# Where the last loads of a one-core transformer layer land, and how its token tiles are finished

## The chip, the core and the metric

The kernel runs on one core of one Trainium2 chip. The time is the device time of one execution in microseconds (us), the median of three runs. The core has five engines that run their own instruction streams and wait for each other through semaphores: TensorE (PE, with its weight loads shown as PEld), VectorE (DVE), ScalarE (ACT), GpSimd (POOL) and SyncE (SP). SP and POOL issue nearly all transfers here, ACT a few. SBUF is the on-chip memory, PSUM the banks that TensorE writes to.

## The reference

One layer of a decoder: RMSNorm, one wide input projection, sparse attention and a gated MLP side by side, two projections up, an output projection, and at the end a gate with a per-layer embedding and a final RMSNorm. S is 512 tokens, D is 2048. What matters here is the end:

```python
x = x + merged @ w_out[l]
x = x + jax.nn.sigmoid(x @ w_ple_gate[l]) * (p[l] @ w_ple[l])
return rms_norm(x, final_g)          # x * rsqrt(mean(x*x)) * final_g
```

The matrix `w_ple_gate` is 2048 x 2048. Call x after the output projection x2, and p[l] @ w_ple the embedding term. The final norm needs the sum of squares of a whole row of 2048, so no part of a row can be written out before all four column groups of that row are there.

## The kernel before, in words

**Numbers as sums.** Matmuls run on pairs: every fp32 operand is split into a high part, rounded for TensorE, and a low part, the rest (`high` at L141 on ACT, `low` at L147 on DVE). One product of two tiles is three matmuls: high x high, high x low, low x high.

**Jobs.** All weight matmuls are a list of jobs that one generator, `gemm`, yields through matmul by matmul. The weights stream from HBM through a ring of three buffers named `raw` (512 KB each, two row blocks of 128); SP issues a load when the buffer's last reader, a `low` on DVE, is done. Before each step of a job `gemm` calls `flush` (work put off by one step), `split_to` (the splits of weights of coming steps) and `pop`. `pop` takes items from a queue `background`; how many per step is `state["pops"]`. So the order of DVE, ACT and POOL instructions among the splits is fixed by these queues when the program is built.

**The last three jobs** multiply x2 by `w_ple_gate`: `pg0` gives column group 0 of the gate (512 columns), `pg1` groups 1 and 2, `pg3`, the last job, group 3. `pg3` has 16 row blocks. Its first eight go step by step over all four token tiles (128 tokens each; lines L349 to L351). Its last eight, the *tail*, are kept whole in SBUF in tiles named `th` and `tl`, and the tail's matmuls (L366 to L368) run token tile by token tile: tile t=0 takes its 24 matmuls, then t=1, and so on. So the four token tiles finish one after the other, and `evac_last(ps, t)` is called when tile t is there.

**The gate and the final norm.** For a column group cg and token tile t, `ple_add` (L701 and L704) makes x2 + 0.5 (1 + tanh) embedding with two DVE instructions; a Square on ACT (L724, or L743 for group 3) adds up the squares. For groups 0, 1 and 2 this is `final_add(cg, t)`, an item of `background`. Group 3 is done in `evac_last`: tanh out of PSUM (L736), sums of the squares of the other groups (L739, L740), `ple_add`, Square, a Sqrt on ACT (L749), a reciprocal on DVE (L751), and then the four column groups are multiplied by that factor and by `final_g` and stored. Tanh and Sqrt need different function tables on ACT; a one-element activation on `warm` (L738, L765) loads the table ahead of use.

In the kernel before, t=0 and t=1 are finished together, after t=1 has come; they multiply by the factor and `final_g` in one DVE instruction per piece (L756). For t=2 and t=3 the multiplication by `final_g` (the tile `fg`) is done ahead of time: groups 0, 1 and 2 by POOL (`final_weigh`, L728, six calls), group 3 by DVE (L745); what is left is the factor alone (L762 on DVE, L759 on ACT).

**Late loads.** While `pg3` runs, five tiles of 1 MB each are loaded by POOL's queue: the x2 of groups 1 and 3, the embedding terms of groups 1 and 3, and `final_g`, one row of 8 KB repeated over the 128 partitions. Places: `fq` is a pool that is opened when the pool of job `pg1` closes. It holds `fg`, the x2 of groups 1 and 3 and the tail; the embedding of group 1 goes to the tile `x`, that of group 3 to a tile `s4` that group 0 has used. One item, `load_last`, issues three of the loads; it stands behind the four `final_add(2, t)`.

With one pop per step, the items are taken in this order: `final_add(2, 0..3)`, `load_last`, `final_add(1, 0..3)`, six `final_weigh`.

Of the kernel before, what the change touches and what calls it, by code (L numbers as in the profile page):

```python
# [13 lines left out]
F32 = mybir.dt.float32  # L14
F32R = mybir.dt.float32r
BF16 = mybir.dt.bfloat16
AF = mybir.ActivationFunctionType
ALU = mybir.AluOpType
# [3 lines left out]
P = 128  # L22
S = 512
D = 2048
TT = S // P
# [38 lines left out]
def kernel(ctx: ExitStack, tc: tile.TileContext, x, p, norm_g, w_in,  # L64
                      pe_k, w1_k, w2_k, pe_v, w1_v, w2_v, ln_g, ln_b, sgu_w, sgu_b,
                      w_up_a, w_up_b, w_out, w_ple, w_ple_gate, final_g, out):
    nc = tc.nc
    x, out = x[0], out[0]
    p = p[0, 0]
# [15 lines left out]
    eps_t = const.tile([P, 1], F32, name="eps_t")  # L85
    nc.gpsimd.memset(eps_t, EPS)
    warm = const.tile([P, 1], F32, name="warm")
# [74 lines left out]
    background = deque()  # L162
# [43 lines left out]
    state = {"loads": 0, "sum": 0, "high": 0, "low": 0, "ahead": 0, "more": 1, "pops": 2, "due": 0}  # L206
# [178 lines left out]
    def finish(name):  # L385
        while name not in done:
            next(run)
        flush()
# [95 lines left out]
    pl_in, ple_t = {}, {}  # L484
# [17 lines left out]
    def spilled(cg):  # L502
        return spill[:, 512 * cg:512 * cg + 512].rearrange("(t p) c -> p t c", p=P)
# [190 lines left out]
    f_tiles, x2_tiles, sg_tiles = {}, {}, {}  # L694
    ss = small[:, 48:64].rearrange("p (t c) -> p t c", t=TT)

    def place(tag, dtype):
        return actp.tile([P, 4, S], dtype, tag=tag, name="p_" + tag)

    def ple_add(cg, t, sg):  # L700
        nc.vector.scalar_tensor_tensor(out=sg, in0=sg, scalar=1.0, in1=ple_t[cg][:, t],  # L701
                                       op0=ALU.add, op1=ALU.mult)
        sl = x2_tiles[cg][:, t]
        nc.vector.scalar_tensor_tensor(out=sl, in0=sg, scalar=0.5, in1=sl, op0=ALU.mult, op1=ALU.add)  # L704
        return sl
# [15 lines left out]
    def final_add(cg, t):  # L721

        sl = ple_add(cg, t, sg_tiles[cg][:, t])
        deferred.append(lambda: nc.scalar.activation(sg_tiles[cg][:, t], sl, AF.Square, accum_out=ss[:, t, cg:cg + 1]))  # L724

    def final_weigh(cg, t):
        sl = x2_tiles[cg][:, t]
        nc.gpsimd.tensor_tensor(out=sl, in0=sl, in1=f_tiles["fg"][:, 512 * cg:512 * cg + 512], op=ALU.mult)  # L728

    def evac_last(ps, t):  # L730
        fg = f_tiles["fg"]
        if t == 0:
            f_tiles["rs"] = f_tiles["pool"].tile([P, TT, 2], F32, name="rs")
        r = f_tiles["rs"]
        sg = stream.tile([P, 512], F32, tag="hi", name="sg", bufs=4)
        nc.scalar.activation(sg, ps[t], AF.Tanh, scale=0.5)  # L736
        if t:
            nc.scalar.activation(warm, eps_t, AF.Sqrt)  # L738
        nc.vector.tensor_reduce(out=r[:, t, 0:1], in_=ss[:, t, 0:3], axis=AX.X, op=ALU.add)  # L739
        nc.vector.tensor_scalar(out=r[:, t, 0:1], in0=r[:, t, 0:1], scalar1=1.0 / D, scalar2=EPS,  # L740
                                op0=ALU.mult, op1=ALU.add)
        sl = ple_add(3, t, sg)
        nc.scalar.activation(sg, sl, AF.Square, accum_out=ss[:, t, 3:4])  # L743
        if t > 1:
            nc.vector.tensor_tensor(out=sl, in0=sl, in1=fg[:, 1536:], op=ALU.mult)  # L745
        if t == 0:
            return
        for i in range(0 if t == 1 else t, t + 1):
            nc.scalar.activation(r[:, i, 1:2], ss[:, i, 3:4], AF.Sqrt, bias=r[:, i, 0:1], scale=1.0 / D)  # L749
            rs = r[:, i, 0:1]  # L750
            nc.vector.reciprocal(rs, r[:, i, 1:2])  # L751
            for cg in (0, 2, 1, 3):
                c = slice(512 * cg, 512 * cg + 512)
                rows, o = out[i * P:i * P + P, c], x2_tiles[cg][:, i]
                if i < 2:
                    nc.vector.scalar_tensor_tensor(out=o, in0=o, scalar=rs, in1=fg[:, c], op0=ALU.mult, op1=ALU.mult)  # L756
                    nc.sync.dma_start(rows, o)
                elif t == TT - 1 and cg < 2:
                    nc.scalar.mul(o, o, rs)  # L759
                    nc.scalar.dma_start(rows, o)  # L760
                else:
                    nc.vector.tensor_scalar(out=o, in0=o, scalar1=rs, scalar2=None, op0=ALU.mult)  # L762
                    nc.sync.dma_start(rows, o)
        if t < TT - 1:
            nc.scalar.activation(warm, eps_t, AF.Tanh)  # L765

    def gate_act(p, k, t):
# [6 lines left out]
    add_job(Job("pg0", "N", w_ple_gate, 0, 512, KT, h_act, evac_first, zs))  # L774
    add_job(Job("pg1", "S", w_ple_gate, 512, 512, KT, gate_act, evac_quad(final_sg, place_sg), ("o", "s", "t")))
    add_job(Job("pg3", "N", w_ple_gate, 1536, 512, KT, h_act, evac_last, ("s", "s", "g", "g"), tail=8))

    run = gemm()
# [115 lines left out]
    with tc.tile_pool(name="cmp", bufs=1) as cmp:  # L894
# [32 lines left out]
        for m in range(16):  # L927
            o, st, sp = hid[m // 8], m % 8 == 0, m % 8 == 7
# [10 lines left out]
        t = o32[:, 4, 128:256].rearrange("p (g n) -> p g n", g=GROUPS)  # L939
        h = o32[:, 5].rearrange("p (g r n) -> p g r n", g=GROUPS, r=4)  # L940
        c = cmp.tile([P, 1], F32, name="hid_c")
        lo_r, up_r = slice(0, 64), slice(64, 128)
        for n, rows in enumerate((lo_r, up_r)):
            o, q = (t[rows].rearrange("p (s g n) -> p s g n", s=2, g=GROUPS)[:, n]
                    for t in (o32[:, 6, :8 * (NCMP + 2)], hid[1]))
            nc.vector.tensor_tensor(out=c[rows], in0=o[:, 0, NCMP:NCMP + 1], in1=q[:, 0, NCMP + 1:], op=ALU.add)
            nc.vector.scalar_tensor_tensor(out=y[rows], in0=o[:, :, :NCMP], scalar=c[rows], in1=q[:, :, 1:NCMP + 1],
                                           op0=ALU.add, op1=ALU.add)
# [374 lines left out]
    for hf in range(2):  # L1323
        b = bank("s", "ps_w")
        for j in range(4):
            nc.tensor.transpose(b[:, j * P:j * P + P], wn[hf][:, j], ident)
        nc.vector.tensor_tensor(out=ws[hf], in0=b.rearrange("p (g t) -> p g t", g=4),
                                in1=tri.unsqueeze(1).to_broadcast([P, 4, P]), op=ALU.mult)
# [9 lines left out]
    def new_s4(q, dtype=F32R):  # L1338
        t = s4p.tile([P, 4, S], dtype, tag=f"s4{q}", name=f"s4{q}")
        return t  # L1340
# [116 lines left out]
    def new_x(dtype=F32):  # L1457
        t = xp.tile([P, 4, S], dtype, tag="x", name="x")
        return t
# [55 lines left out]
    def columns(src, cg):  # L1515
        return src[:, 512 * cg:512 * cg + 512].rearrange("(t p) c -> p t c", p=P)
# [124 lines left out]
    def load_x2(cg, t):  # L1641
        x2_tiles[cg] = t
        nc.gpsimd.dma_start(t, columns(x2_dram, cg))

    def load_ple(cg, t):
        ple_t[cg] = t
        nc.gpsimd.dma_start(t, spilled(cg))
# [16 lines left out]
        flush()  # L1664
    ph_q.close()
    fq = f_tiles["pool"] = ctx.enter_context(tc.tile_pool(name="fq", bufs=1))
    fg = f_tiles["fg"] = fq.tile([P, D], F32, name="fg")
    tails = {i: fq.tile([P, 8, 512], F32R, name="t" + i) for i in "hl"}
    f_tiles["tail"] = lambda i, k: tails[i][:, k:k + 1]
    assert not background  # L1670
    for cg, t in ((1, new_x()), (3, new_s4(0, F32))):
        ple_t[cg] = t
    late = {cg: fq.tile([P, TT, 512], F32, name=f"x2_{cg}") for cg in (1, 3)}
    load_x2(1, late[1])
    load_ple(1, ple_t[1])
    state["pops"] = 1

    def load_last():
        nc.gpsimd.dma_start(fg, bass.AP(tensor=final_g.tensor, offset=final_g.offset, ap=[[0, P], [1, D]]))
        load_ple(3, ple_t[3])  # L1680
        load_x2(3, late[3])

    background.extend(lambda t=t: final_add(2, t) for t in range(TT))
    background.append(load_last)
    background.extend(lambda t=t: final_add(1, t) for t in range(TT))
    background.extend(lambda t=t, cg=cg: final_weigh(cg, t) for t in (2, 3) for cg in range(3))
    finish("pg3")


# [23 lines left out]
```

## Time and profile before

| | us |
|---|---|
| median of three runs | 1570.96 (1570.68 to 1571.43) |
| the profiled execution: its time | 1571.01 |
| its span | 1569.3 |
| TensorE busy | 1549.3 (99%) |
| VectorE busy | 1164.2 (74%) |
| ScalarE busy | 770.4 (49%) |
| GpSimd busy | 231.3 (15%) |

All times of instructions below are in us from the start of the span. A line of a timeline gives the start, the duration, the engine, the kernel's line, the operation, what it writes and reads, how many instructions are merged in the row, and in brackets how long the engine had been idle and who released it. In the trace, tiles carry the name of the first tile in their place: `p_l` is the x2 of groups 0 and 2 (which places `l3` and `l2` hold), `p_h` the tanh of groups 1 and 2, `s` and `x` the embeddings or the x2, `sg` the tanh of group 3. `raw<-in_w_ple_gate_dram` is a weight load. In the table of stages, the columns are the stretch, its length, and the busy time of each engine in it with the number of instructions, then TensorE's clock, the busy share of the DMA engines and what they moved.

### The profile page before, as it was taken

The numbers are of one execution on the slowest core, as the hardware profiler recorded it, in microseconds if no ns is written. First come the engines' busy times: TensorE is split into PE (matmuls) and PEld (weight loads), VectorE is DVE, ScalarE is ACT, GpSimd is POOL, SyncE is SP. The second block draws the span as 40 slices with busy tenths as digits, with TensorE's granted clock in tenths as the row PEclk, the third lists the DMA queues.
The fourth block names the chain that finished last, engine by engine and source line by source line (L and its number), as shares of the span: only waits on it lengthen the run. The fifth ranks groups of instructions, "written<-read, shape, count | busy, mean of one in ns | idle before, by whom it ended". The sixth has DMA issues, their size and how long they took to land.

```text
span 1569.3 us, 20475 instructions
## 1 busy us (share of the span) xinstructions
PE 1549.3 (99%) x7486; PEld 1296.5 (83%) x7486; DVE 1164.2 (74%) x1854; ACT 770.4 (49%) x1334; POOL 231.3 (15%) x351
## 2 busy tenths in 40 slices
PE   9999999999999999999999999999999999999995
PEld 7889988888888888888888888888888888888884
DVE  6543358888886977878887777777665687888876
ACT  6433346667664545445544444455323344444545
POOL 1200000101022520001121212210031121100111
PEclk9999999999999999999999999999999999999998
DMA  8423431212124993517473737674832496555572
GB/s 316 130 81 86 113 81 42 55 41 55 41 55 117 291 295 84 206 54 241 135 263 104 270 102 250 233 261 166 304 114 92 134 281 215 172 175 175 184 254 113
DMA packets 158164, 250.35 MB, mean 160 GB/s; under 512 B 8664, under 2 KB 82032, under 8 KB 156016
## 3 DMA queue, kind: packets, MB, share of 16 engines
q1 hardware_dynamic: 116080, 149.84, 30.8%
q0 software_dynamic: 41696, 98.69, 18.9%
q8 instruction: 59, 0.97, 0.3%
q10 hardware_dynamic: 288, 0.52, 0.1%
q14 instruction: 41, 0.34, 0.1%
HBM read 199.21 MB, written 49.81 MB: 159 GB/s over the span
## 4 chain that ended last, share of the span: by engine, by line
PE 93%; DVE 3%; DMA 1%; ACT 1%; issue 0%; SPq 0%; POOL 0%; ACTq 0%; DVEq 0%; POOLq 0%
PE ps_m L311 6%; PE ps_m L312 6%; PE ps_m L313 6%; PE ps_t L1042 2%; PE ps_za L337 2%; PE ps_za L339 2%; PE ps_za L338 2%; PE ps_u L349 2%; PE ps_u L350 2%; PE ps_u L351 2%; PE ps_ub L351 2%; PE ps_ub L350 2%; PE ps_wo L349 2%; PE ps_wo L351 2%; PE ps_wo L350 2%; PE ps_ub L349 2%
## 5 line engine op out<-in xcount | busy, mean ns | idle before, releaser
L147 DVE TENSOR_TENSOR ls<-b,hs 128x1024 fp32r<-128x1024 f32 x180 | 220.3, 1224 | 119.2 <-ACT hs L141 118.3
L141 ACT CAST hs<-b 128x1024 fp32r<-128x1024 f32 x180 | 189.2, 1052 | 213.4 <-PE ps_m L313 86.0
L147 DVE TENSOR_TENSOR lo<-raw,hi 128x512 fp32r<-128x512 f32 (+1 forms) x248 | 172.9, 703 | 112.0 <-issue 27.2
L141 ACT CAST hi<-raw 128x512 fp32r<-128x512 f32 (+1 forms) x248 | 149.5, 608 | 189.9 <-PE ps_ub L351 46.4
L141 ACT CAST hs<-raw 128x1024 fp32r<-128x1024 f32 x72 | 75.9, 1054 | 88.8 <-PE ps_m L313 35.7
L147 DVE TENSOR_TENSOR ls<-raw,hs 128x1024 fp32r<-128x1024 f32 x72 | 88.0, 1222 | 16.8 <-ACT hs L141 16.7
L311 PE MATMUL ps_m<-hs,act_h 128*128 128x512 f32 x256 | 100.5, 392 | 0.0
L312 PE MATMUL ps_m<-ls,act_h 128*128 128x512 f32 x256 | 99.7, 389 | 0.0
L313 PE MATMUL ps_m<-hs,act_l 128*128 128x512 f32 x256 | 99.7, 389 | 0.0
L240 DVE TENSOR_TENSOR b<-b,b 128x1024 f32<-128x1024 f32 x72 | 87.7, 1218 | 0.0
L240 DVE TENSOR_TENSOR b<-raw,b 128x1024 f32<-128x1024 f32 x72 | 87.7, 1217 | 0.0
L141 ACT CAST pth<-ps_t 128x512 fp32r<-128x512 f32 (+1 forms) x88 | 48.0, 545 | 65.6 <-PE ps_t L1042 65.3
L1003 ACT ACTIVATE prob<-prob,st 128x512 f32<-128x512 f32 (+3 forms) x128 | 70.7, 555 | 3.9 <-DVE st L994 3.8
L147 DVE TENSOR_TENSOR ptl<-ps_t,pth 128x512 fp32r<-128x512 f32 (+1 forms) x88 | 56.2, 639 | 21.2 <-ACT pth L141 20.3
L994 DVE CUSTOM_DVE_ANT_0 prob<-ps_s,b 128x512 f32<-128x512 f32 (+3 forms) x128 | 56.3, 486 | 10.0 <-PE ps_s L991 9.8
L313 PEld LDWEIGHTS ps_m<-hs,act_l 128*128 128x128 f32 x256 | 48.0, 188 | 10.1
L311 PEld LDWEIGHTS ps_m<-hs,act_h 128*128 128x128 f32 x256 | 48.1, 188 | 9.7
L312 PEld LDWEIGHTS ps_m<-ls,act_h 128*128 128x128 f32 x256 | 48.1, 188 | 9.7
L337 PE MATMUL ps_za<-act_h,hi 128*128 128x512 f32 x128 | 55.8, 436 | 0.0
L337 PE MATMUL ps_q<-act_h,hi 128*128 128x512 f32 x128 | 53.7, 419 | 0.0
L1042 PEld LDWEIGHTS ps_t<-ident,prob 128*128 128x128 f32 x320 | 39.7, 140 | 13.9 <-DVE ptl L147 2.8
L1042 PE MATMUL ps_t<-ident,prob 128*128 128x128 f32 x320 | 49.5, 273 | 1.3 <-DVE ptl L147 1.2
(588 smaller groups left out, 4382.0 us busy)
## 6 DMA issues: line engine op xcount, KB each, us to landing
raw<-in_w_in_dram SPq DMA_DIRECT2D x116, 512.0 KB, 3.9
b<-in_w_in_dram SPq DMA_DIRECT2D x48, 512.0 KB, 5.4
raw<-in_w_out_dram SPq DMA_DIRECT2D x24, 512.0 KB, 4.4
raw<-in_w_ple_gate_dram SPq DMA_DIRECT2D x24, 512.0 KB, 4.2
raw<-in_w_up_b_dram SPq DMA_DIRECT2D x16, 512.0 KB, 4.0
oa_d<-oa POOLq DMA_DIRECT2D x28, 256.0 KB, 4.8
gate<-keep POOLq DMA_DIRECT2D x24, 256.0 KB, 3.8
xt<-in_x_dram SPq DMA_DIRECT2D x4, 1024.0 KB, 11.1
```

Of the source, the lines that this page charges most:

```text
L141: nc.scalar.copy(hi, src)
L147: nc.vector.tensor_tensor(out=lo, in0=src, in1=hi.bitcast(F32), op=ALU.subtract)
L240: nc.vector.tensor_tensor(out=b[o], in0=b[x], in1=b[y], op=ALU.subtract)
L311: nc.tensor.matmul(o, ah, hi[:, i], start=st, stop=False, skip_group_check=go)
L312: nc.tensor.matmul(o, ah, lo[:, i], start=False, stop=False, skip_group_check=go)
L313: nc.tensor.matmul(o, al, hi[:, i], start=False, stop=sp, skip_group_check=go)
L337: nc.tensor.matmul(ps, hi[:, j], ah, start=st, stop=False)
L349: nc.tensor.matmul(o, ah[:, sl], hi[:, j], start=st, stop=False)
L350: nc.tensor.matmul(o, ah[:, sl], lo[:, j], start=False, stop=False)
L351: nc.tensor.matmul(o, al[:, sl], hi[:, j], start=False, stop=sp)
L1003: nc.scalar.activation(sl, sl, AF.Exp, bias=st[:, 0, j, hh:hh + 1], scale=-1.0, accum_out=st[:, 1, j, hh:hh + 1])
L1042: nc.tensor.transpose(b[:, (2 * e + hh) * P:(2 * e + hh + 1) * P], pts[hh][:, c:c + P], ident)
```

## The change

Three things, all in the last job:

- **Places and time of the late loads.** `fg` no longer has a place of its own in `fq`; nor has the x2 of group 3. The embedding of group 1 gets a place in `fq` in their stead. The embedding of group 3 goes to the place of group 2's embedding, the x2 of group 3 to the place of group 2's tanh (`h3`), `final_g` to the place of group 1's tanh (`h2`). Each of these three comes free only when the `final_add` of that group, its Square included, is done. `final_g` is loaded by an item of its own, `load_weights`, behind all of `final_add(1, t)`.
- **Two items per step.** `pops` is 2, with three empty items `nothing` as padding. The order is now: `final_add(2, 0..3)`, nothing, `load_last`, `final_add(1, 0..3)`, nothing, nothing, `load_weights`, three `final_weigh` (t=3 alone).
- **Each token tile is finished by itself.** t=0, 1 and 2 each load the Sqrt table, take their own factor, and do the multiplication by factor and `final_g` in one DVE instruction per piece; t=3 is as before.

```diff
-        if t:
-            nc.scalar.activation(warm, eps_t, AF.Sqrt)
+        nc.scalar.activation(warm, eps_t, AF.Sqrt)
...
-        if t > 1:
+        last = t == TT - 1
+        if last:
             nc.vector.tensor_tensor(out=sl, in0=sl, in1=fg[:, 1536:], op=ALU.mult)
-        if t == 0:
-            return
-        for i in range(0 if t == 1 else t, t + 1):
-            nc.scalar.activation(r[:, i, 1:2], ss[:, i, 3:4], AF.Sqrt, bias=r[:, i, 0:1], scale=1.0 / D)
...
+        nc.scalar.activation(r[:, t, 1:2], ss[:, t, 3:4], AF.Sqrt, bias=r[:, t, 0:1], scale=1.0 / D)
+        rs = r[:, t, 0:1]
+        nc.vector.reciprocal(rs, r[:, t, 1:2])
+        for cg in (0, 2, 1, 3):
+            c = slice(512 * cg, 512 * cg + 512)
+            rows, o = out[t * P:t * P + P, c], x2_tiles[cg][:, t]
+            if not last:
+                nc.vector.scalar_tensor_tensor(out=o, in0=o, scalar=rs, in1=fg[:, c], op0=ALU.mult, op1=ALU.mult)
+                nc.sync.dma_start(rows, o)
+            elif cg < 2:
+                nc.scalar.mul(o, o, rs)
+                nc.scalar.dma_start(rows, o)
+            else:
+                nc.vector.tensor_scalar(out=o, in0=o, scalar1=rs, scalar2=None, op0=ALU.mult)
+                nc.sync.dma_start(rows, o)
+        if not last:
             nc.scalar.activation(warm, eps_t, AF.Tanh)
...
-    fg = f_tiles["fg"] = fq.tile([P, D], F32, name="fg")
...
-    for cg, t in ((1, new_x()), (3, new_s4(0, F32))):
-        ple_t[cg] = t
-    late = {cg: fq.tile([P, TT, 512], F32, name=f"x2_{cg}") for cg in (1, 3)}
-    load_x2(1, late[1])
-    load_ple(1, ple_t[1])
-    state["pops"] = 1
+    load_x2(1, fq.tile([P, TT, 512], F32, name="x2_1"))
+    load_ple(1, fq.tile([P, TT, 512], F32, name="ple_1"))
+    state["pops"] = 2
 
     def load_last():
+        load_ple(3, new_s4(1, F32))
+        load_x2(3, place("h3", F32))
+
+    def load_weights():
+        fg = f_tiles["fg"] = place("h2", F32).rearrange("p a s -> p (a s)")
         nc.gpsimd.dma_start(fg, bass.AP(tensor=final_g.tensor, offset=final_g.offset, ap=[[0, P], [1, D]]))
-        load_ple(3, ple_t[3])
-        load_x2(3, late[3])
 
     background.extend(lambda t=t: final_add(2, t) for t in range(TT))
-    background.append(load_last)
+    background.extend([nothing, load_last])
     background.extend(lambda t=t: final_add(1, t) for t in range(TT))
-    background.extend(lambda t=t, cg=cg: final_weigh(cg, t) for t in (2, 3) for cg in range(3))
+    background.extend([nothing, nothing, load_weights])
+    background.extend(lambda cg=cg: final_weigh(cg, TT - 1) for cg in range(3))
```

More of the change, by code (lines that the diff above doesn't have):

```diff
@@ L743, in evac_last @@
         nc.scalar.activation(sg, sl, AF.Square, accum_out=ss[:, t, 3:4])
-        if t > 1:
+        last = t == TT - 1
+        if last:
             nc.vector.tensor_tensor(out=sl, in0=sl, in1=fg[:, 1536:], op=ALU.mult)
-        if t == 0:
-            return
-        for i in range(0 if t == 1 else t, t + 1):
[L749 to L764, printed above, removed]
+        nc.scalar.activation(r[:, t, 1:2], ss[:, t, 3:4], AF.Sqrt, bias=r[:, t, 0:1], scale=1.0 / D)
[14 more added lines that the diff above has]
+        if not last:
             nc.scalar.activation(warm, eps_t, AF.Tanh)
```

## The prediction, made before the changed kernel was run

> **What bounds the kernel now.** I read the page first, for the span and the busiest engine, then the table of stages for the last 50 us, then the timelines of TensorE, DVE, ACT and POOL there, and the list of transfers.
>
> ```profile
> span 1569.3 us, 20475 instructions
> PE 1549.3 (99%) x7486; PEld 1296.5 (83%) x7486; DVE 1164.2 (74%) x1854; ACT 770.4 (49%) x1334; POOL 231.3 (15%) x351
> ```
>
> TensorE is busy for 99%, and its list of matmuls is the same in both kernels, so only two things can move: holes in TensorE's work in the last job, and the time between its last matmul and the end. The table of stages shows both.
>
> ```profile
> 1520.00:1530.00 10.00, 10.00 (x45) 8.27 (x45) 7.06 (x10) 4.24 (x9) 1.29 (x1) 1.00 1.02 403
> 1530.00:1540.00 10.00, 8.81 (x37) 6.57 (x36) 7.71 (x13) 4.34 (x10) 0.44 (x1) 1.00 0.06 22
> ...
> 1550.00:1560.00 10.00, 4.51 (x20) 3.39 (x19) 9.00 (x20) 6.15 (x12) 0.00 (x0) 0.85 0.57 220
> 1560.00:1570.00 10.00, 0.00 (x0) 0.00 (x0) 3.22 (x9) 3.77 (x7) 0.00 (x0) 0.50 0.52 200
> ```
>
> Up to 1530 the DMA engines are full (403 GB/s), and right after it TensorE has its only hole. From 1554.5 on TensorE has nothing left, and DVE (9.00 of 10) and ACT finish the token tiles. TensorE's timeline gives the hole its size.
>
> ```profile
> 1530.70 0.39 PE L366 MATMUL ps_pg<-th,ob_l 128*128 128x512 f32 x1
> ...
> 1535.52 0.50 PE L367 MATMUL ps_pg<-tl,act_h 128*128 128x512 f32 x1 [0.23 <-DVE tl L147]
> 1537.44 0.50 PE L367 MATMUL ps_pg<-tl,act_h 128*128 128x512 f32 x1 [0.96 <-DVE tl L147]
> 1538.01 0.40 PE L366 MATMUL ps_pg<-th,ob_l 128*128 128x512 f32 x1
> ...
> 1554.12 0.39 PE L368 MATMUL ps_pg<-th,act_l 128*128 128x512 f32 x1
> ```
>
> From 1538.01 (first of t=1) to 1554.12 (last of t=3) lie 71 steps, so a matmul starts every 0.227. Tile t=0, from 1530.70, should take 24 x 0.227 = 5.44 and end its turn at 1536.14; t=1 starts at 1538.01. The hole is 1.9 us. It waits for `tl`, and the chain says why `tl` is late:
>
> ```profile
> 1523.31 7.47 DMA raw<-in_w_ple_gate_dram
> ```
>
> A 512 KB weight load needed 7.47 because five late tiles of 1 MB were queued since 1512.
>
> **Term 1: the hole.** The change issues two of the five at first, two after `final_add(2, 3)` and its Square, the last after that of `final_add(1, 3)`. DVE and ACT then run in this order: split 7 (`lo`), split 8 (`tl`), two `final_add(1)`, splits 9 and 10, two `final_add(1)`, splits 11 to 15. Prices come from these rows.
>
> ```profile
> 1522.59 0.69 DVE L147 TENSOR_TENSOR lo<-raw,hi 128x512 fp32r<-128x512 f32 x1 [0.72 <-PE ps_pg L350]
> ...
> 1525.14 0.68 DVE L701 SCALAR_TENSOR_TENSOR p_h<-p_h,s 128x512 f32<-128x512 f32 x1
> 1525.85 0.69 DVE L704 SCALAR_TENSOR_TENSOR p_l<-p_h,p_l 128x512 f32<-128x512 f32 x1
> 1526.46 0.68 DVE L147 TENSOR_TENSOR tl<-raw,th 128x512 fp32r<-128x512 f32 x1
> ```
> ```profile
> 1526.58 0.64 ACT L724 ACTIVATE p_h<-p_l 128x512 f32<-128x512 f32 x1 [2.22 <-DVE p_l L704]
> ```
>
> A `final_add` occupies DVE for 1.32 (1525.14 to 1526.46), and a split, of L704's shape, for 0.61 to the next instruction; Square holds ACT for 0.64. Split 7 stays at 1522.59, since TensorE releases it. Then: split 8 at 1523.2; additions to 1526.45; split 9; Square and `th` of 10 on ACT put split 10 at 1527.85; additions to 1531.1; split 11; the last Square from 1531.2 and `th` of 12 put split 12 at 1532.5; 13, 14, 15 follow at 0.61, the last ends at 1535.0. TensorE wants the low part of 15 at 1530.70 + 22 x 0.227 = 1535.7. Margin 0.5 to 0.7 for the last four, so the hole goes, if the weights are there.
>
> ```profile
> raw<-in_w_ple_gate_dram SPq DMA_DIRECT2D x1, 512.0 KB, 4.9
> ...
> p_l<-x_d POOLq DMA_DIRECT2D x1, 1024.0 KB, 5.4
> ...
> fg<-in_final_g_dram POOLq DMA_DIRECT2D x1, 1024.0 KB, 10.9
> ...
> x<-x_d POOLq DMA_DIRECT2D x1, 1024.0 KB, 16.9
> ```
>
> They should be. At 0.4 MB per us, the first two tiles and one weight load (2.5 MB) are in by 1518; the next two, issued about 1517 and 1519, with one weight load, by 1526. SP issues the last weight load when split 9 is done, at 1527.2; the row of 4.9 is that load in this trace, while others still ran: 1532.1, needed at 1532.9. SP's queue is passed by nothing else; POOL's queue holds, behind its waits, only `final_g` and three `final_weigh`. Bounds: 0 to 1.9 of the hole stay; I take 0, worth **-1.9**. The early additions (two per step) delay splits 3 and 5 by about 0.3 and 0.5, which the ring of three `lo` tiles hides; without it that 0.5 would be TensorE's.
>
> **Term 2: the finish.** These rows price one token tile.
>
> ```profile
> 1541.32 1.68 DVE L701 SCALAR_TENSOR_TENSOR sg<-sg,s 128x512 f32<-128x512 f32 x1 [1.02 <-ACT sg L736]
> 1543.03 1.67 DVE L704 SCALAR_TENSOR_TENSOR x<-sg,x 128x512 f32<-128x512 f32 x1
> ...
> 1549.56 1.41 DVE L756 SCALAR_TENSOR_TENSOR p_l<-p_l,rs,fg 128x512 f32<-128x512 f32 x2
> 1550.89 1.41 DVE L756 SCALAR_TENSOR_TENSOR x<-x,rs,fg 128x512 f32<-128x512 f32 x2
> 1552.21 0.16 DVE L751 RECIPROCAL rs<-rs 128x1 f32<-128x1 f32 x1
> ...
> 1555.06 0.15 DVE L739 TENSOR_REDUCE rs<-small 128x1 f32<-128x3 f32 x1
> ...
> 1555.32 0.68 DVE L701 SCALAR_TENSOR_TENSOR sg<-sg,s 128x512 f32<-128x512 f32 x1
> ...
> 1560.23 0.68 DVE L701 SCALAR_TENSOR_TENSOR sg<-sg,s 128x512 f32<-128x512 f32 x1
> ```
> ```profile
> 1540.71 0.58 ACT L736 ACTIVATE sg<-ps_pg 128x512 f32<-128x512 f32 x1
> ...
> 1545.96 1.28 ACT L738 ACT_TABLE_LOAD   x1
> 1547.25 0.20 ACT L738 ACTIVATE warm<-eps_t 128x1 f32<-128x1 f32 x1
> ...
> 1556.76 0.63 ACT L743 ACTIVATE sg<-x 128x512 f32<-128x512 f32 x1 [3.73 <-DVE x L704]
> ...
> 1557.51 0.29 ACT L749 ACTIVATE rs<-small,rs 128x1 f32<-128x1 f32 x1
> 1557.83 1.28 ACT L765 ACT_TABLE_LOAD   x1
> ...
> 1559.23 0.58 ACT L736 ACTIVATE sg<-ps_pg 128x512 f32<-128x512 f32 x1
> ```
>
> One tile on DVE: sums to Square's start 1.70 (1555.06 to 1556.76), Square 0.75, Sqrt 0.29, reciprocal 0.22 with its hand-over, four pieces 2.65 (1549.56 to 1552.21): 5.61, more than TensorE's 5.44, so DVE sets the beat. ACT in the same cycle: tanh 0.60, switch to Sqrt 1.40 (as from 1557.83 to 1559.23), Square 0.75, Sqrt 0.32, switch to Tanh 1.40: 4.47, beside DVE's work. The change adds one pair of switches, at t=0; the Sqrt switch runs while DVE does L701 and L704 (1.4), the Tanh switch under the four pieces. If that cover went, a switch would cost 1.4 each. For t=2 the four pieces cost 2.65 in place of L745 and four bare multiplications; the 5.61 holds that.
>
> Start: tile t=0 leaves TensorE at 1530.70 + 23 x 0.227 + 0.39 = 1536.3. ACT is free, since the additions are done. In the trace tanh of t=0 began at 1540.71 and L701 0.61 later; now L701 starts at 1536.9. Three beats later, L701 of t=3 starts at 1536.9 + 16.8 = 1553.8. In the trace it starts at 1560.23. From there on t=3 is unchanged (9.1 to the span's end).
>
> **Term 3: POOL against DVE.** The three `final_weigh` wait for `final_g`. Its load is issued when the last Square ends (1532.2); alone in the queues it should take the 5.4 of the x2 row, so 1537.6. The first piece wants it at 1539.6.
>
> ```profile
> 1541.16 2.99 POOL L728 TENSOR_TENSOR p_l<-p_l,fg 128x512 f32<-128x512 f32 x2
> ...
> 1545.82 1.28 POOL L728 TENSOR_TENSOR p_l<-p_l,fg 128x512 f32<-128x512 f32 x1
> ```
>
> L701 and L704 took 1.68 and 1.67 beside these, 0.68 alone: a DVE instruction that meets a POOL one loses 1.0 to 1.28 (POOL's own length). From 1537.6 POOL works to about 1542; the first of the three or the second falls into DVE's wait for Square and Sqrt, so two meet DVE: +2.2. Bounds 0 and 3 x 1.28 = 3.8.
>
> **Sum.** L701 of t=3 at 1553.8 + 2.2 = 1556.0, 4.2 before 1560.23. The profiled execution took 1571.01, 0.05 over the median of the runs: 1571.0 - 4.2 = **1566.8**, 0.27% less.
>
> **The rivals.**
> *The hole stays*, now from the order of DVE and ACT: one Square or `th` 0.5 late pushes all later splits. For it: the small margin. Against it: every wait in that chain is priced from a row. Time: 1566.8 + 1.9 = 1568.7.
> *`final_g` is slow by itself.* It took 10.9 in the trace. If that is its own pace (one row read 128 times), it lands at 1543.1, 3.5 after the first piece wants it, and all three POOL instructions meet the pieces (3.3): 6.8 in place of 2.2, 1571.4, no change. Against it: in the trace it stood behind 2 MB.
> *Slower: the late load waits in the queues.* The last of the five took 16.9. With that, `final_g` comes at 1549.1: 9.5 + 3.3 in place of 2.2, 1577.4. It decides, beyond +3.1, from a landing at 1545.9 on, 13.7 after issue. Against it: from 1532 nothing else is queued.
> *Table switches set the beat.* If a switch cost 1.28 more than its rows, ACT's cycle would be 7.0, and Square of t=3 would start at 1536.3 + 21.0 + 3.3 = 1560.6, where the trace has it about 1561.7 (1560.23 + 1.44): 1570.0. Against it: `warm` starts 0.01 after the load's end. The Trainium skill's ScalarE: Activation LUTs, What ACT_TABLE_LOAD costs, has such a cost: a drain of about 1.38 us on top of 1.283 at every switch. By that rule this change would come out near 1570.6 (an estimate); the trace agrees with the 1.28 and shows no drain.
>
> **How the numbers follow.** Forecast 0.62 (1565.0 to 1567.8, by POOL's two ends and some tenths of margin lost); hole stays 0.14; `final_g` slow 0.10; slower 0.06; switches 0.02; something I do not see in the same few us 0.06, split evenly. A measurement tells 0.2% (3.1 us) from no change. Faster: 0.62 + 0.02; within 0.2%: 0.14 + 0.10 + 0.02 + 0.02 = 0.28; slower: 0.06 + 0.02. The range from 1565.0 to 1570.2 holds the forecast, the hole that stays, alone and with a `final_g` that comes 1.5 late, and the switches: about 0.8. The forecast's own is 1565.0 to 1567.8.
>
> **What would show it.** Right: no idle time before L366 to L368, TensorE's last matmul near 1552.2, tanh of t=0 near 1536.3, `final_g` landing near 1537.6, the four pieces of t=0 longer than 2.65 by about 2, then tiles 5.6 apart. Wrong: waits of TensorE for `tl`, DVE waiting for `final_g` at t=0, or tiles more than 6 apart after t=0.

## The result, and the profile after

The changed kernel takes 1566.20 us (median of 8 runs, 1566.09 to 1566.41); the kernel before took 1570.86 beside it (8 runs, 1570.19 to 1571.43). The ratio is 0.9971, with a 95% interval from 0.9960 to 0.9982: 4.7 us or 0.3% faster. The profiled execution took 1566.09.

The page of the changed kernel:

```profile
span 1564.4 us, 20473 instructions
PE 1547.8 (99%) x7486; PEld 1296.3 (83%) x7486; DVE 1163.1 (74%) x1853; ACT 773.2 (49%) x1338; POOL 227.6 (15%) x348
```

The span is 4.9 shorter. The table of stages shows where (columns as before: the stretch, then TensorE, its weight loads, DVE, ACT, POOL, the clock, the share of the DMA engines, GB/s):

```profile
1520.00:1530.00 10.00, 10.00 (x45) 8.26 (x44) 7.14 (x12) 4.33 (x11) 0.00 (x0) 1.00 0.88 327
1530.00:1540.00 10.00, 10.00 (x46) 8.28 (x45) 6.37 (x10) 6.01 (x14) 3.83 (x3) 1.00 0.29 105
...
1550.00:1560.00 10.00, 2.15 (x10) 1.45 (x8) 7.13 (x15) 6.72 (x14) 0.00 (x0) 0.77 0.41 156
```

From 1530 to 1540 TensorE is busy for 10.00, where it was busy for 8.81: the hole is gone. The transfers that filled the DMA engines until 1530 (403 GB/s) now reach into the next stretch (327 and 105). TensorE's timeline, with the first matmul of t=0, the first of t=1 and the last of the kernel:

```profile
1530.23 0.39 PE L366 MATMUL ps_pg<-th,ob_l 128*128 128x512 f32 x1
...
1535.67 0.39 PE L366 MATMUL ps_pg<-th,ob_l 128*128 128x512 f32 x1
...
1551.76 0.39 PE L368 MATMUL ps_pg<-th,act_l 128*128 128x512 f32 x1
```

Tile t=0 takes 5.44, which is 24 steps without a wait. The first of these matmuls began at 1530.70 in the trace before, so the new trace is 0.47 ahead before the hole could show. It is there long before the last job and ahead of every late load (a split on ACT at 1339.22, against 1339.69, and the first tanh of `pg1` at 1507.99, against 1508.46). I count it as a difference between two executions, not as a gain: the kernel with pieces held back, further below, has the changed kernel's program up to there, and its first tanh of `pg1` comes at 1508.41. The last matmul is 2.36 earlier: 0.47, and 1.89 of the hole. DVE's timeline from the last splits on:

```profile
1532.01 2.50 DVE L147 TENSOR_TENSOR tl<-raw,th 128x512 fp32r<-128x512 f32 x4 [0.70 <-ACT th L141]
...
1536.56 0.69 DVE L701 SCALAR_TENSOR_TENSOR sg<-sg,s 128x512 f32<-128x512 f32 x1 [1.79 <-ACT sg L736]
1537.29 1.66 DVE L704 SCALAR_TENSOR_TENSOR p_h<-sg,p_h 128x512 f32<-128x512 f32 x1
1540.06 0.16 DVE L748 RECIPROCAL rs<-rs 128x1 f32<-128x1 f32 x1 [1.12 <-ACT rs L746]
1540.26 2.30 DVE L753 SCALAR_TENSOR_TENSOR p_l<-p_l,rs,p_h 128x512 f32<-128x512 f32 x2
...
1544.05 0.68 DVE L701 SCALAR_TENSOR_TENSOR sg<-sg,s 128x512 f32<-128x512 f32 x1
...
1549.69 0.68 DVE L701 SCALAR_TENSOR_TENSOR sg<-sg,s 128x512 f32<-128x512 f32 x1
...
1555.33 0.68 DVE L701 SCALAR_TENSOR_TENSOR sg<-sg,s 128x512 f32<-128x512 f32 x1
```

The four L701 mark the four token tiles: 1536.56, 1544.05, 1549.69, 1555.33, so beats of 7.49, 5.64 and 5.64. ACT at t=0:

```profile
1535.93 0.60 ACT L736 ACTIVATE sg<-ps_pg 128x512 f32<-128x512 f32 x1 [2.38 <-PE ps_pg L368]
1536.54 1.28 ACT L737 ACT_TABLE_LOAD   x1
1537.84 0.20 ACT L737 ACTIVATE warm<-eps_t 128x1 f32<-128x1 f32 x1
```

The tanh of t=0 waits for TensorE, for 2.38, and starts 0.1 after that tile's last matmul (the one ahead of 1535.67, at 1535.44, and 0.39 long). Before, it stood behind the Squares of group 1 and began at 1540.71, 2.5 after the end of t=0's last matmul (the one ahead of 1538.01 in the trace before, at 1537.78, and 0.39 long). POOL, and the landings of its late loads:

```profile
1516.86 0.75 POOL L1644 DMA_DIRECT2D s<-spill  x1 [6.21 <-DVE p_h L701]
1518.34 0.75 POOL L1640 DMA_DIRECT2D p_h<-x_d  x1 [0.73 <-ACT p_h L724]
1531.76 0.55 POOL L1677 DMA_DIRECT2D p_h<-in_final_g_dram  x1 [12.68 <-ACT p_h L724]
1536.71 1.68 POOL L728 TENSOR_TENSOR p_l<-p_l,p_h 128x512 f32<-128x512 f32 x1 [4.40 <-DMA p_h<-in_final_g_dram]
1538.37 1.73 POOL L728 TENSOR_TENSOR x<-x,p_h 128x512 f32<-128x512 f32 x1
1540.06 1.29 POOL L728 TENSOR_TENSOR p_l<-p_l,p_h 128x512 f32<-128x512 f32 x1
```
```profile
s<-spill POOLq DMA_DIRECT2D x1, 1024.0 KB, 5.4
p_h<-x_d POOLq DMA_DIRECT2D x1, 1024.0 KB, 8.4
p_h<-in_final_g_dram POOLq DMA_DIRECT2D x1, 1024.0 KB, 4.9
```

So the 4.9 of the two spans comes apart like this: 0.47 was there before; L701 of t=0 starts 4.76 earlier, 4.29 of it from the last job; from there to L701 of t=3 it takes 18.77, against 18.91 before (1541.32 to 1560.23); and from L701 of t=3 to the end of the span 9.07, as before. Nearly the whole gain is the earlier start of t=0: 1.9 from the hole and 2.4 from a tanh that no longer stands behind additions. The finish itself is hardly shorter in sum.

### The profile page after: what moved, and what is told of

Its sections match the earlier page's. It is cut to its first block, busy times and chain, and to the rows that moved or that the text cites. A ratio compares the mean times of both kernels' runs of the same rounds, so it can differ in the third digit from the quotient of the medians.

```text
span 1564.4 us, 20473 instructions
## 1 busy us (share of the span) xinstructions
PE 1547.8 (99%) x7486; PEld 1296.3 (83%) x7486; DVE 1163.1 (74%) x1853; ACT 773.2 (49%) x1338; POOL 227.6 (15%) x348
## 4 chain that ended last, share of the span: by engine, by line
PE 95%; DVE 3%; ACT 1%; issue 0%; POOL 0%; ACTq 0%; POOLq 0%; DVEq 0%
PE ps_m L311 7%; PE ps_m L313 7%; PE ps_m L312 6%; PE ps_za L337 2%; PE ps_za L339 2%; PE ps_t L1039 2%; PE ps_za L338 2%; PE ps_u L349 2%; PE ps_u L350 2%; PE ps_wo L350 2%; PE ps_ub L349 2%; PE ps_ub L350 2%; PE ps_ub L351 2%; PE ps_wo L351 2%; PE ps_wo L349 2%; PE ps_u L351 2%
```

## The experiments

The questions were: which of the three parts carries the gain; what POOL's three multiplications cost; and what bounds the finish now. Times are medians; the first four kernels were run beside the kernel before at 1570.52 (28 runs), the last three beside it at 1571.22 (9 runs), and the changed kernel as told above. The first four undo one part, or make one alone; the diffs are shortened and start from the changed kernel:

| kernel | places | items per step | finish | time | ratio to before, 95% |
|---|---|---|---|---|---|
| finish alone | old | 1 | new | 1570.19 | 0.9999 (0.9990 to 1.0007) |
| old finish | new | 2 | old | 1567.79 | 0.9982 (0.9973 to 0.9991) |
| old places | old | 2 | new | 1567.34 | 0.9979 (0.9970 to 0.9988) |
| one per step | new | 1 | new | 1575.24 | 1.0030 (1.0019 to 1.0042) |
| all three (the change) | new | 2 | new | 1566.20 | 0.9971 (0.9960 to 0.9982) |

**The old finish with the new loads and order.**

```diff
 def evac_last(ps, t):          # as before: t=0 and t=1 together, t=2 and t=3 weighed ahead
...
-    background.extend(lambda cg=cg: final_weigh(cg, TT - 1) for cg in range(3))
+    background.extend(lambda t=t, cg=cg: final_weigh(cg, t) for t in (2, 3) for cg in range(3))
```

> The late loads and the two additions per step as in the changed kernel, the finish of the token tiles as in the kernel before (t=0 and t=1 together, six final_weigh). Theory: the hole of TensorE is gone and tanh of t=0 starts as early as in the changed kernel (about 1536), but the batch of eight pieces after t=1 and three more POOL multiplications, which now run after the landing of final_g, put L701 of t=3 about 3 us later than in the changed kernel: 1569.2 us. Rival: the finish by itself gives nothing, since from L701 of t=0 to L701 of t=3 it took 18.9 us before and 18.8 us after: 1566.3 us.

It took 1567.79 (1567.41 to 1568.20, 11 runs), between the two expectations. DVE and, in the second fence, ACT:

```profile
1536.69 0.69 DVE L701 SCALAR_TENSOR_TENSOR sg<-sg,s 128x512 f32<-128x512 f32 x1 [1.79 <-ACT sg L736]
...
1542.13 1.14 DVE L701 SCALAR_TENSOR_TENSOR sg<-sg,s 128x512 f32<-128x512 f32 x1 [2.80 <-ACT sg L736]
1543.31 1.66 DVE L704 SCALAR_TENSOR_TENSOR p_h<-sg,p_h 128x512 f32<-128x512 f32 x1
...
1551.91 0.68 DVE L701 SCALAR_TENSOR_TENSOR sg<-sg,s 128x512 f32<-128x512 f32 x1
...
1556.82 0.68 DVE L701 SCALAR_TENSOR_TENSOR sg<-sg,s 128x512 f32<-128x512 f32 x1
```
```profile
1541.50 0.60 ACT L736 ACTIVATE sg<-ps_pg 128x512 f32<-128x512 f32 x1 [1.66 <-PE ps_pg L368]
```

The hole stays away and t=0 starts at 1536.69, so the loads and the order bring that start without the new finish. Then DVE stands idle for 2.80, since t=0 is not finished before t=1 has come out of TensorE. L701 of t=3 comes at 1556.82: from that of t=0 it takes 20.13, against the changed kernel's 18.77. I had expected about 3 more, from six POOL multiplications instead of three. But much of POOL's work fell into that idle time, and of t=1's instructions only two met POOL (1.14 and 1.66, where 0.68 and 0.69 are the length alone); and t=2, whose pieces need only the factor, took 4.91 (1551.91 to 1556.82) in place of 5.64. The new finish is worth 1.4 by the traces here; by the times, whose intervals overlap, it is no more than likely.

**The finish alone.**

```diff
-    state["pops"] = 2
+    state["pops"] = 1
...                             # loads, places and items as before; new evac_last
     background.extend(lambda cg=cg: final_weigh(cg, TT - 1) for cg in range(3))
```

> Only the finish tile by tile; loads, places and one item per step as in the kernel before. Theory: the hole of 1.9 us stays, and tanh of t=0 waits for the additions of group 1 until about 1540.7 as before; three beats of 5.6 and one or two meetings with POOL from there: L701 of t=3 near 1559.5, time 1570.2 us, 0.7 less than before. Rival: the finish carries the gain, then 1567 us or less.

It took 1570.19 (1569.23 to 1571.67, 11 runs): no change, as expected. DVE's first and last L701, and what TensorE waited for in the last 50 us:

```profile
1540.69 1.40 DVE L701 SCALAR_TENSOR_TENSOR sg<-sg,s 128x512 f32<-128x512 f32 x1 [1.03 <-ACT sg L736]
...
1559.28 0.68 DVE L701 SCALAR_TENSOR_TENSOR sg<-sg,s 128x512 f32<-128x512 f32 x1
```
```profile
PEld ps_pg L367 <- DVE tl L147: 1.6, 2, 1.4
...
PE ps_pg L367 <- DVE tl L147: 1.0, 1, 1.0
```

The hole is still there, t=0 starts at 1540.69, and from L701 of t=0 to that of t=3 it takes 18.59, against 18.91 before. TensorE's last matmul starts at 1553.49 here, so t=1 is there at 1553.49 - 48 x 0.227 + 0.39 = 1543.0, and t=0's second instruction ends only at 1543.8: nothing is gained by not waiting for t=1. The first two tiles take 12.95 in place of 14.00, with two meetings with POOL in place of three, and t=2 takes 5.64 in place of 4.91, since its pieces are no longer multiplied ahead of time. The new finish pays only behind the earlier start.

**One item per step, with the new places.**

```diff
-    state["pops"] = 2
+    state["pops"] = 1
```

> The changed kernel with one item per step in place of two: places and finish as there. Theory: the places tie the loads to the additions, so that later additions make later loads. The hole stays away, but the additions of group 1 end about 4 us later, tanh of t=0 starts near 1539, final_g is issued near 1539.5, lands near 1544.5, and the pieces of t=0 wait 2 us for it and meet POOL three times: about 1572 us, slower than before. Rival: the places alone take the queue off the weights, the order does not matter: 1566 to 1567 us.

It took 1575.24 (1574.68 to 1575.74, 6 runs), slower than the kernel before by 0.3%, and 3 beyond what I had expected. POOL's issues, what ACT waited for, and DVE:

```profile
1524.35 0.75 POOL L1644 DMA_DIRECT2D s<-spill  x1 [13.65 <-DVE p_h L701]
...
1541.97 0.55 POOL L1677 DMA_DIRECT2D p_h<-in_final_g_dram  x1 [15.39 <-ACT p_h L724]
```
```profile
ACT th L141 <- DMA raw<-in_w_ple_gate_dram: 6.0, 1, 6.0
```
```profile
1534.31 0.69 DVE L147 TENSOR_TENSOR tl<-raw,th 128x512 fp32r<-128x512 f32 x1 [5.74 <-ACT th L141]
...
1547.33 3.50 DVE L753 SCALAR_TENSOR_TENSOR p_l<-p_l,rs,p_h 128x512 f32<-128x512 f32 x2 [2.43 <-DMA p_h<-in_final_g_dram]
```

The two gated loads go out 7.5 later than in the changed kernel (1524.35 against 1516.86) and now lie beside the last weight load, which is issued at 1525.4 and takes 8.2: ACT waits 6.0 for it, and the last splits come so late that the hole returns (TensorE's turn of t=0 takes 7.29 in place of 5.44). I had expected the hole to stay away here, and that is refuted. The tanh of t=0 starts at 1541.58, where I had expected 1539; that is most of the 3. `final_g`, issued at 1541.97 after the last Square, lands 5.3 later, and the first pieces wait 2.43 for it and then meet POOL. Places that come free late tie the loads to the additions; with additions as late as before, that is a loss.

**The old places, with two items per step and the new finish.**

```diff
+    fg = f_tiles["fg"] = fq.tile([P, D], F32, name="fg")
...                             # embedding and x2 in places of their own, as before
     def load_last():
-        load_ple(3, new_s4(1, F32))
-        load_x2(3, place("h3", F32))
-
-    def load_weights():
-        fg = f_tiles["fg"] = place("h2", F32).rearrange("p a s -> p (a s)")
         nc.gpsimd.dma_start(fg, ...)
+        load_ple(3, ple_t[3])
+        load_x2(3, late[3])
...
-    background.extend([nothing, nothing, load_weights])
+    background.extend([nothing, nothing, nothing])
```

> The changed kernel's order (two per step) and finish, with the places of the kernel before, so that all five late tiles are issued by 1514. Theory: the weights come late again (blocks 12 and 13 near 1530.8), and the POOL multiplications, no longer held back by final_g, meet the splits of the tail: a hole of about 2 us in TensorE, but none of the 1.9 us that POOL costs the pieces of t=0; 1566.5 us, within 1 us of the changed kernel. Rival: the places are what pays, the hole comes on top of everything else: 1568.1 us or more.

It took 1567.34 (1566.57 to 1568.38, 11 runs), 1.1 over the changed kernel's median, a little more than the 1 that I had expected at most; the intervals overlap, the traces differ clearly. First a row of the changed kernel, DVE's first split of the tail, for comparison, then DVE, POOL and the waits of this kernel:

```profile
1522.72 0.68 DVE L147 TENSOR_TENSOR tl<-raw,th 128x512 fp32r<-128x512 f32 x1
```
```profile
1524.42 0.69 DVE L147 TENSOR_TENSOR tl<-raw,th 128x512 fp32r<-128x512 f32 x1 [1.49 <-ACT th L141]
...
1533.72 4.26 DVE L147 TENSOR_TENSOR tl<-raw,th 128x512 fp32r<-128x512 f32 x4 [0.70 <-ACT th L141]
...
1539.67 0.69 DVE L701 SCALAR_TENSOR_TENSOR sg<-sg,s 128x512 f32<-128x512 f32 x1 [1.43 <-ACT sg L736]
```
```profile
1533.26 1.28 POOL L728 TENSOR_TENSOR x<-x,fg 128x512 f32<-128x512 f32 x1 [9.18 <-ACT p_h L724]
1534.51 1.73 POOL L728 TENSOR_TENSOR p_l<-p_l,fg 128x512 f32<-128x512 f32 x1
```
```profile
ACT th L141 <- DMA raw<-in_w_ple_gate_dram: 3.4, 1, 3.4
...
PEld ps_pg L367 <- DVE tl L147: 3.1, 3, 1.2
...
PE ps_pg L367 <- DVE tl L147: 1.9, 3, 0.9
```

Two things lengthen the splits. ACT waits 3.4 for a weight load, with all five late loads issued by 1513.4, and the first split of the tail comes 1.7 later than in the changed kernel. And `final_g` is there early, so POOL multiplies as soon as the Squares allow, at 1533.26 and 1534.51, and meets the last four splits: 4.26 for four, where the changed kernel needs 2.50. The four end 3.5 later in all, and TensorE's last matmul starts at 1554.87, 3.1 later (0.1 of each is an offset that this trace has from before the tail): a hole of 3, where I had expected 2. L701 of t=0 comes at 1539.67. In return POOL is done when the finish begins, all three beats are 5.64, and L701 of t=3 comes at 1556.59, only 1.26 after the changed kernel's. So the late places do not take POOL's meetings away, they move them from the splits, where TensorE waits, to the finish, where DVE waits; what they save in the end is about 1 us, by times whose intervals overlap. Two items per step and the new finish bring the larger part of the gain.

**No multiplication ahead of time.**

```diff
-    background.extend(lambda cg=cg: final_weigh(cg, TT - 1) for cg in range(3))
```

> The changed kernel without the three final_weigh on POOL; left out is the multiplication by final_g of groups 0, 1 and 2 of the last token tile. Theory: POOL's meetings with DVE delay t=0 by 1.9 us, and DVE sets the beat from there to the end, so all of it comes back: 1564.3 us. Rival: the delay is hidden behind TensorE, which still works until 1552: 1566.2 us.

It took 1564.50 (1564.08 to 1564.91, 5 runs); ratio 0.9957 (0.9944 to 0.9969), 2.2 below the changed kernel by the ratios (0.0014 x 1571), as expected; the two intervals overlap a little, the ranges of the times lie apart (1564.91 at most, against 1566.09 at least). DVE:

```profile
1536.65 0.69 DVE L701 SCALAR_TENSOR_TENSOR sg<-sg,s 128x512 f32<-128x512 f32 x1 [1.79 <-ACT sg L736]
1537.38 0.69 DVE L704 SCALAR_TENSOR_TENSOR p_h<-sg,p_h 128x512 f32<-128x512 f32 x1
...
1542.30 0.68 DVE L701 SCALAR_TENSOR_TENSOR sg<-sg,s 128x512 f32<-128x512 f32 x1
...
1553.57 0.68 DVE L701 SCALAR_TENSOR_TENSOR sg<-sg,s 128x512 f32<-128x512 f32 x1
```

L704 of t=0 takes 0.69 in place of 1.66, the first beat is 5.65 in place of 7.49, and the others are as they were. This measures the third term of the sum by itself: 1.84.

**Pieces held back into the wait for Square and Sqrt.** Each tile has DVE idle for 1.12 ahead of its reciprocal. Here the last two pieces of a tile (of t=2 the last one) are put off into that time of the next tile, which reorders DVE's work and takes none of it away.

```diff
+        while held:                  # behind the Square of the next tile
+            held.pop(0)()
...
+                if cg == 3 or (cg == 1 and t < TT - 2):
+                    held.append(piece)
+                else:
+                    piece()
```

> The changed kernel; of the four pieces of a token tile the last two (for t=2 the last one) are put off and done in the next tile while DVE waits for Square and Sqrt. Theory: DVE sets the beat of 5.6 us, with 1.1 us in it in which it waits for ACT; filled, its beat falls below TensorE's 5.44, and t=3 starts when TensorE is done: L701 of t=3 near 1552.9 in place of 1555.3, 1563.9 us. Rival: ACT with its table switches or TensorE is the bound of the finish: 1566 us.

It took 1563.74 (1563.30 to 1564.15, 5 runs); ratio 0.9952 (0.9939 to 0.9966), as expected. DVE at t=2 and t=3, then ACT at t=3:

```profile
1547.81 0.69 DVE L701 SCALAR_TENSOR_TENSOR sg<-sg,s 128x512 f32<-128x512 f32 x1
...
1553.24 0.69 DVE L701 SCALAR_TENSOR_TENSOR sg<-sg,s 128x512 f32<-128x512 f32 x1 [0.26 <-ACT sg L738]
```
```profile
1552.61 0.60 ACT L738 ACTIVATE sg<-ps_pg 128x512 f32<-128x512 f32 x1 [0.79 <-PE ps_pg L368]
```

Now DVE waits for the tanh of t=3 and that tanh for TensorE's last matmul: TensorE sets the finish, and POOL's meetings at t=0 are absorbed. L701 of t=3 comes at 1553.24, and at 1552.82 without the 0.42 that this trace is behind the changed kernel's from before the tail; 1552.9 was expected. This shows that in the changed kernel DVE set the beat, and that its idle 1.12 per tile was usable.

**A shorter last tile, on top of that.**

```diff
-        if last:
-            nc.vector.tensor_tensor(out=sl, in0=sl, in1=fg[:, 1536:], op=ALU.mult)
...
-            elif cg < 2:
+            elif cg == 0:            # on ACT; groups 1 and 2 on DVE, group 3 by factor and final_g in one
```

> As the kernel with pieces put off, and the last tile divided otherwise: no separate multiplication of group 3 by final_g ahead of the reciprocal, group 3 in one instruction with the factor, three groups on DVE and one on ACT in place of two and two. Theory: the reciprocal comes 0.3 us earlier and the last transfer is issued 0.4 us earlier after it: 0.7 us less, 1563.2 us. Rival: the end is set by the transfers, which share the DMA engines: no change against the kernel with pieces put off.

It took 1563.48 (1563.14 to 1564.15, 5 runs); ratio 0.9951 (0.9939 to 0.9964). That is 0.26 under the kernel above with ranges that overlap; five runs don't tell the two apart, and it is less than half of the 0.7 that I had expected. In the traces, from L701 of t=3 to the end of the span it takes 8.77 against 9.06. The reciprocal comes 0.29 sooner behind that L701, and the last store is issued 0.62 sooner (4.38 against 5.00), about as forecast; only 0.29 of it reaches the end, and no run here shows why. Both kernels beat the kernel before clearly, and the changed one by 2.5 and 2.7 in the medians and 3 by the ratios; the ranges of the times lie apart (1564.15 at most, against 1566.09 at least), the intervals of the ratios overlap a little.

## Why the prediction was right

The forecast was 1566.8, the time 1566.2. Positions are compared after 0.47 has been added to the new trace, the offset that it had from long before the last job.

- *Term 1, the hole goes, -1.9.* Right: 1.89. The chain of splits came as it was added up: split 8 at 1523.19 (1523.2 was forecast), split 12 at 1532.48 (1532.5), the end of split 15 at 1534.98 (1535.0). TensorE's low part of split 15 was due at 1535.68 (1530.70 + 22 x 0.227), which leaves the margin of 0.7. The gated loads were issued at 1517.33 and 1518.81 (1517 and 1519); the row of the first says that it waited for L701, the last reader of group 2's embedding, and not for the Square, as I had written of all three gated loads. The margin is real and small: with the old places splits that came 3.4 late made a hole of 3. One reading was loose: the five late loads of the trace before were not all queued at 1512, but issued from 1509.63 to 1513.70; no term rests on that.
- *Term 2, the start.* Right: L701 of t=0 at 1537.03 (1536.9). Its reason, that ACT is free then, holds as well: the tanh waited for TensorE and for nothing on its own engine.
- *Term 2, the beat of 5.61, set by DVE.* Right: 5.64, and the experiment with held pieces shows that it was DVE's order, not TensorE's pace, that set it.
- *Term 3, POOL against DVE, +2.2.* The mechanism was right, the size was too large: 1.85 (7.49 less 5.64), and 1.84 with POOL's work left out. Two instructions of DVE met POOL, as forecast, L704 (1.66, 0.97 lost) and the first piece (2.30 for two pieces where two take 1.41, 0.89 lost); the second POOL multiplication lay mostly in DVE's wait. Taking 1.1 for each was what failed. The rows that the prediction showed had a loss of 1.0 each, and 1.28, POOL's whole length, was met by neither; DVE's piece came 0.2 into the POOL instruction and waited for what was left of it. `final_g` landed 4.9 after its issue, 0.5 sooner than the 5.4 taken.
- *The sum.* L701 of t=3 at 1555.80 (1556.0), then 9.07 (9.1). The last job gave 4.43, against 4.2; the other 0.47 between the spans was no part of the change.

The rivals. *The hole stays*: not here. *`final_g` is slow by itself*: no, 4.9 alone; the 10.9 in the trace before came with 2 MB ahead of it, and so did 10.4 in the kernel with the old places. *Late in the queues*: not here; with one item per step a late load did make the kernel slower, but by waiting for its place and beside a weight load, not behind others in POOL's queue. *Switches set the beat*: no. At t=0 the load starts 0.01 after the tanh's end and `warm` 0.02 after the load's end, and the beat behind two switches is 5.64. The Trainium skill (ScalarE: Activation LUTs, What ACT_TABLE_LOAD costs) gives each switch a further drain of about 1.38 us; the trace shows its load of 1.28 and none of that drain, and the measurement decides.

What the prediction did not say is how the gain is shared: finishing each tile by itself, which was priced inside the beats, is worth nothing that the runs can tell without the earlier start, and the late places gain about 1 with two items per step and lose 5.0 with one (1575.24 against 1570.19). Neither the places nor the order closes the hole alone: it is 1.9 with one item per step, and 3 with the old places. The prediction priced the three only together. Two items per step alone, with the old places and the old finish, was not run. What stays open too is whether the last tile's shorter order is worth its 0.3, and how the 1.4 of the old finish splits between idle time of DVE and POOL's meetings.

## What to carry to other kernels

When the end of a kernel is a chain of tiles, write down for each tile when its input comes, how long its busiest engine needs, and what stands ahead of its first instruction in that engine's queue: here the work queued ahead of the first tile cost more than TensorE's hole (2.4 against 1.9), and how each tile was finished made no difference that could be measured until that was gone. Before tying a load to a place that comes free late, look at when it comes free and which other load then lies beside it; the same places gained about 1 us with early additions and lost 5 with late ones. And where an engine idles for one short wait per tile, as DVE here for 1.12, moving two independent instructions into it can be worth more than rearranging the loads (2.5 here, with POOL's meetings absorbed, against 1).

## What the hardware showed that was not expected

DVE and POOL took turns by whole instructions, and both pay; the prediction had priced DVE's side alone. Where POOL was at a two-input multiplication, DVE's L704 took 1.66 in place of 0.69; where DVE had come first, POOL's took 1.68 and 1.73 in place of 1.29. With splits it was the same: four took 4.26 in place of 2.50. That is what the Trainium skill states (SBUF — State Buffer, Who interferes with whom): a two-input DVE instruction and a POOL instruction that reads SBUF share a read port, and the one that comes second waits until the first is done. The trace agrees, and adds the price here: three POOL multiplications of 1.29 cost the other engine 1.85, because one of them fell into its wait.

A load on POOL's queue goes out when its place is free, not where it stands among the items. The three loads of `load_last` stand behind four additions in the list, but with places that no addition holds (the kernel with the old places) they were all issued by 1513.4; only the places of the changed kernel (1516.86, 1518.34 and 1531.76) tie them to the additions.
